# Scan in fixed steps with operands a step ahead, and full-row low products of rotated queries

## The chip, the cores and the metric

The kernel runs on one core of one Trainium2 chip. The time is the device time of one execution in microseconds (us), and the figure given for a kernel is the median of several runs. The engines of the core are named as in the profile: PE is TensorE (PEld is its weight load), DVE is VectorE, ACT is ScalarE, POOL is GpSimd, SP is the queue on which this kernel issues all its DMAs.

## The reference, cut to what matters

One encoder layer is applied to two sequences, of 512 and 1024 rows (1536 in all), of width 1024, in float32. Each has an attention branch with 8 heads (128 columns without and 64 with a rotary turn) and a bidirectional state-space scan with 32 heads in 4 groups, in chunks of 128 rows. The two parts that the change touches are these:

```python
# scan, once forward and once on the flipped sequence; per chunk c, group g, head e of the group
a_cum = jnp.cumsum(a, axis=2)
diff = acl[..., :, None] - acl[..., None, :]
Lm = jnp.exp(jnp.where(tri, diff, -jnp.inf))
CB = jnp.einsum('bclgn,bcsgn->bcgls', Cc, Bc)
y_diag = jnp.einsum('bcgls,bcgels,bcsgep->bclgep', CB, Lm, xdt)
states = jnp.einsum('bclgn,bclge,bclgep->bcgepn', Bc, decay_states, xdt)
hstate = dec * hstate + st                     # from chunk to chunk
y_off = jnp.einsum('bclgn,bcgepn,bclge->bclgep', Cc, prev, jnp.exp(a_cum))
y = y_diag + y_off + xf * D
# attention scores, per head and block of 128 queries
q = concat([q[..., :128], rope(q[..., 128:])]);  k = concat([k[..., :128], rope(k[..., 128:])])
sc = einsum('bqhd,bkhd->bhqk', q, k) * scale;  p = softmax(sc)
```

## The kernel before

Matrix products are made from a high part and a low part of each operand (`fp32r`): `mm3` (L91) issues high by high, high by low and low by high. The work runs in these stages: a start up to some 90 us, then for each of the four groups g the input products and a convolution (`conv_block`), **the scan of the group**, and the products of the gate z (`zev`); then **attention** from some 1640 us to 2260 us; then the output products.

The scan of a group (L616 to L785) has four phases. `prepass` goes backward over the chunks of the first sequence and stores each backward state in DRAM (`sbD`); `mainpass` goes forward over its 4 chunks in steps of half a chunk (4 heads, index u), 8 steps; in between, and after, `prepass` of the second sequence; then `mainpass` of the second sequence, 8 chunks in 16 steps. A step of `mainpass` holds:

- `head`: loads a chunk's transposed rows `xb` and backward state `sb`, makes the product of B and C in PSUM (`sm`) and masks it twice on DVE into `cu`.
- `weights`: two DMAs bring rows of cumulated decays (`ab`), POOL subtracts (L704, L705), ACT scales `cu` eight times (L710, L711), DVE adds, picks by a mask (L713), ACT takes the exponential (L714), DVE multiplies (L715) into `wt`.
- `products`: eight products of `wt` into `py`, one step after `weights`.
- `state` and `follow`: DVE weighs the chunk (`tmp`), ACT and POOL make high and low parts (POOL L685, L687), and a step later PE multiplies them (`mm3` into `sm`) and DVE advances the forward state `stf`.
- `decays` and `carried`: DMAs of `eb` and its exponential on ACT (L662); a step later the states times C (L673, into `sm`), multiplied by `eb` on DVE (L674).
- `tail`: DVE adds `py` and `eb` into `xs`.

All small PSUM results share the three buffers `sm`. Between steps `feed(FEED)` issues independent work, the *filler*: windows of 24 products of the input projection (`mm<-hH,wh`, lines L92 to L94) that the attention and output stages need later; 18 windows in group 0 and 21 in each of the others. A planner orders the instructions of each engine from the order in the program and its own estimate of when operands are ready. The queues are in order on the chip: an instruction that waits holds all that stands behind it on its engine.

In attention, `scores` makes for each block of queries and each 512 keys five products into one PSUM buffer `sp` (L996 to L1000): three `mm3`-like ones of the 128 plain columns, and two of the rotated ones. There the high part `xh` has 128 rows, the 64 rotated columns twice, against `kx`, which holds the high part of the keys in rows 0 to 63 and their low part in rows 64 to 127. The low part `xl` has 64 rows, against rows 0 to 63 of `kx`.

Of the kernel before, what the change touches and what calls it, by code (L numbers as in the profile page):

```python
# [9 lines left out]
F32 = mybir.dt.float32  # L10
# [18 lines left out]
G = 4  # L29
E = 8  # L30
HH = 4
FEED = 0.9
GI = 2
ASC = 0.85
VLAG = 2
HLEAD = 1
FL = 1

ORDER = "l0 a0 n0 l1 a1 m00 n1 w m01 l2 b00 b10 m10 m11 n2 b01 b11 m20 m21 b02 b12"

CUTS = (1, 7, 14, 21, 28)
DOFF = 0
COFF = 1
TH0 = 4
LT0 = 2
AL0 = 1
# [23 lines left out]
def _body(nc, tc, A, O):  # L70
# [232 lines left out]
            pass  # L303

    def tmp(name="tmp"):
        return dict(tmp=pS, ft=pre0).get(name, p1).tile([P, W], F32, name=name, bufs=1 if name == "tmp" else 2)

    free = [kd]

# [264 lines left out]
    for g in range(G):  # L574
# [12 lines left out]
        def tok(c, name, bufs):  # L587

            cs_ = slice(c * P, (c + 1) * P)
            px = smp.tile([P, W], F32, name="sm")  # L590
            for i in range(4):
                PE.transpose(out=px[:, i * P:(i + 1) * P], in_=xs[i][:, cs_], identity=ident)
            pb = smp.tile([P, P], F32, name="sm")
            PE.transpose(out=pb, in_=Bt[:, cs_], identity=ident)
            xb = pS.tile([P, W + P], F32, name=name, bufs=bufs)
            S.copy(xb[:, :W], px)
            S.copy(xb[:, W:], pb)
            return xb
# [15 lines left out]
            return new  # L614

        def prepass(o, n):  # L616
            c0, c1 = o // P, (o + n) // P
            st = None
            for c in range(c1 - 1, c0, -1):
                xb = tok(c, "xp", 1)  # L620
                nc.sync.dma_start(out=xbD[g][c], in_=xb)
                xd = weighted(xb[:, :W], 1, c)
                ps = smp.tile([P, W], F32, name="sm")
                PE.matmul(ps, lhsT=xb[:, W:], rhs=xd, start=True, stop=True)
                st = advance(st, ps, 1, c, p1.tile([P, W], F32, name="raw0", bufs=1) if st is None else st)
                nc.sync.dma_start(out=sbD[g][c - 1], in_=st)
                yield

        def mainpass(o, n):
# [24 lines left out]
            def decays(c):  # L654
                eb = {}
                for d in [0] * (c > c0) + [1] * (c < c1 - 1):
                    eb[d] = pS.tile([P, 4, P], F32, name="eb", bufs=2)
                    r0 = 32 * d + 8 * g
                    for j in range(2):
                        nc.sync.dma_start(out=eb[d][j * 64:j * 64 + 64],  # L660
                                          in_=arD[c][r0:r0 + 8, :].rearrange("(i j) l -> j i l", j=2)[j].partition_broadcast(64))
                    S.activation(eb[d], eb[d], AF.Exp)  # L662
                stt[c]["eb"] = eb

            def carried(c):

                cs_ = slice(c * P, (c + 1) * P)
                eb = stt[c]["eb"]
                for d in sorted(eb):
                    st = stt[c]["sb" if d else "sf"]  # L670
                    ps = smp.tile([P, 4, P], F32, name="sm")
                    for i in range(4):
                        PE.matmul(ps[:, i, :], lhsT=st[:, i * P:(i + 1) * P], rhs=Ct[:, cs_], start=True, stop=True)  # L673
                    V.tensor_tensor(eb[d], eb[d], ps, op=ALU.mult)  # L674
                if len(eb) == 2:
                    V.tensor_tensor(eb[1], eb[1], eb[0], op=ALU.add)
                stt[c]["off"] = eb[max(eb)]
# [16 lines left out]
                    mm3(ps, *stt[c]["parts"], True, True)  # L694
                    sf[0] = advance(sf[0], ps, 0, c, pS.tile([P, W], F32, name="stf", bufs=2))

            def weights(c, u):
                cu = stt[c]["cu"]
                e0 = u * HH
                ab = pS.tile([P, 2, HH, P], F32, name="ab", bufs=3)  # L700
                for d in range(2):
                    r0 = 32 * d + 8 * g + e0
                    nc.sync.dma_start(out=ab[:, d], in_=arD[c][r0:r0 + HH, :].partition_broadcast(P))
                GP.tensor_tensor(ab[:, 0], ab[:, 0], ac_[:, 0, c, e0:e0 + HH].unsqueeze(2).broadcast_to([P, HH, P]), op=ALU.subtract)  # L704
                GP.tensor_tensor(ab[:, 1], ab[:, 1], ac_[:, 1, c, e0:e0 + HH].unsqueeze(2).broadcast_to([P, HH, P]), op=ALU.subtract)  # L705
                wt = pS.tile([P, HH, P], F32, name="wt", bufs=3)
                t1 = pS.tile([P, HH, P], F32, name="t1", bufs=2)
                dc = [[dt_[:, d, c, e0 + e:e0 + e + 1] for e in range(HH)] for d in range(2)]
                for e in range(HH):
                    S.activation(t1[:, e], cu[:, 1, :], AF.Copy, scale=dc[1][e])  # L710
                    S.activation(wt[:, e], cu[:, 0, :], AF.Copy, scale=dc[0][e])  # L711
                V.tensor_tensor(wt, wt, t1, op=ALU.add)
                V.copy_predicated(ab[:, 0], maskb.unsqueeze(1).broadcast_to([P, HH, P]), ab[:, 1])  # L713
                S.activation(ab[:, 0], ab[:, 0], AF.Exp)  # L714
                V.tensor_tensor(wt, ab[:, 0], wt, op=ALU.mult)  # L715
                stt[c, u] = wt

# [19 lines left out]
            for i in range(4):  # L737
                xo = xs[i][:, o:o + n]
                V.tensor_scalar(xo, xo, dsum[:, 4 * g + i:4 * g + i + 1], None, op0=ALU.mult)
            for i in range(len(us) + 1):  # L740
                if i < len(us):
                    c, u = us[i]
                    if u == nu - HLEAD and c + 1 < c1:
                        head(c + 1)
                    weights(c, u)
                    if u == 0:
                        state(c)
                    if u == FL:
                        follow(c)
                    if u == DOFF:  # L750
                        decays(c)
                    if u == COFF:
                        carried(c)
                if i >= 1:
                    c, u = us[i - 1]
                    products(c, u)
                    if u == nu - 1:
                        tail(c)
                yield

        def filling():
# [11 lines left out]
                next(fill, None)  # L773

        for _ in prepass(*SEQS[0]):
            pass
        pre = prepass(*SEQS[1])
        for i, _ in enumerate(mainpass(*SEQS[0])):
            if i % 2:
                next(pre, None)  # L780
            feed(FEED)
        for _ in pre:
            pass
        for _ in mainpass(*SEQS[1]):
            feed(FEED)  # L785
        for _ in fill:
# [168 lines left out]
    def scores(u):  # L955
# [18 lines left out]
        def turn_r():  # L974
            qrw, qrr, rq, rqn = QR[si, hd // 2, w]
            xh = p2.tile([P, W], F32R, name="xh", bufs=2)
            xl = p2.tile([64, W], F32R, name="xl", bufs=2)
            pk = spp.tile([P, W], F32, name="sp")
            for b in range(4):
                PE.transpose(out=pk[:, b * P:(b + 1) * P], in_=qrr[:, b, h], identity=ident)  # L980
            S.copy(xh, pk)
            sub(xl, pk[0:64], r32(xh[0:64]))
            st["x"] = (xh, xl)
            PT[u] = []
            st["su"] = p2.tile([P, nw, 4], F32, name="su", bufs=4)

        def block(b):
            (nh, nl), (xh, xl) = st["n"], st["x"]
            rq, rqn = QR[si, hd // 2, w][2:]
            bs = slice(b * P, (b + 1) * P)  # L990
            sm = p2.tile([P, 8], F32, name="smx", bufs=8)
            sps = []
            for k in range(nw):
                out = spp.tile([P, W], F32, name="sp")
                kh, kl, kx = KV[si, hd, k][:3]
                PE.matmul(out, lhsT=nh[:, bs], rhs=kh, start=True, stop=False)  # L996
                PE.matmul(out, lhsT=nh[:, bs], rhs=kl, start=False, stop=False)  # L997
                PE.matmul(out, lhsT=nl[:, bs], rhs=kh, start=False, stop=False)  # L998
                PE.matmul(out, lhsT=xh[:, bs], rhs=kx, start=False, stop=False)  # L999
                PE.matmul(out, lhsT=xl[:, bs], rhs=kx[0:64], start=False, stop=True)  # L1000
                V.reduce_max(sm[:, k:k + 1], out, axis=AX.X)  # L1001
                sps.append(out)
            if nw == 2:
                V.scalar_tensor_tensor(sm[:, 2:3], sm[:, 0:1], sm[:, 1:2], rqn[:, b, h:h + 1], op0=ALU.max, op1=ALU.mult)  # L1004
            else:
                V.tensor_tensor(sm[:, 2:3], sm[:, 0:1], rqn[:, b, h:h + 1], op=ALU.mult)
            pp = [p2.tile([P, W], F32, name="pp", bufs=10) for _ in range(nw)]
            for k in range(nw):
                S.activation(pp[k], sps[k], AF.Exp, bias=sm[:, 2:3], scale=rq[:, b, h:h + 1], accum_out=st["su"][:, k, b:b + 1])  # L1009
            PT[u].append(pp)  # L1010
# [241 lines left out]
```

## Time and profile before

| | us |
|---|---|
| median of 3 runs | 2793.45 |
| lowest and highest | 2792.09, 2795.47 |
| the profiled execution | 2798.78 |
| its span, first to last instruction | 2797.0 |

The profile is of one execution. Busy time of an engine is the union of its instructions. Matmuls overlap in the pipeline and their ends are modelled, so the distance from the start of one matmul to the start of the next says more of what one costs than its duration.

### The profile page before, as it was taken

Reading aid. Unit: us, or ns where it says so; the run is one execution under the profiler, and the core shown is the slowest. Engines: PE = TensorE matmul, PEld = TensorE weight load, DVE = VectorE, ACT = ScalarE, POOL = GpSimd, SP = SyncE. Lnnn points to the kernel's source line nnn. Section 1 sums busy time; section 2 is a strip of 40 time slices with the busy share of each in tenths; the row PEclk is TensorE's granted clock in tenths of the full one; section 3 lists DMA queues with packets and bytes.
Section 4 is the critical chain, followed back from the end, with each engine's and each line's share of the span. In section 5 each row is a group of like instructions: output and inputs, shape, how many; then the busy total and the mean of one; then the engine's idle time right before and its main releaser. Section 6 shows DMA issues by size and latency. Waiting matters only on the chain. (4 is left out here: it accounts for less than half of the span.)

```text
span 2797.0 us, 36365 instructions
## 1 busy us (share of the span) xinstructions
PE 2658.6 (95%) x12810; PEld 2076.5 (74%) x12810; DVE 1853.7 (66%) x2962; ACT 1323.1 (47%) x2954; POOL 509.0 (18%) x455
## 2 busy tenths in 40 slices
PE   6998889999899998999988999999999999999999
PEld 2786667866778766778667877777777778888887
DVE  5877875788747777567868568776676653466631
ACT  5445554465525555564645356655565552111110
POOL 1003430034300125100224023322221200000000
PEclk9999999999999999999999999999999999999999
DMA  7236652166622366451556222211111142245433
GB/s 245 85 87 180 187 158 96 31 183 193 174 67 83 108 185 176 136 166 42 163 172 169 91 95 86 78 39 41 33 31 31 61 159 94 79 140 162 126 126 102
DMA packets 211206, 325.87 MB, mean 117 GB/s; under 512 B 24816, under 2 KB 74064, under 8 KB 210256
## 3 DMA queue, kind: packets, MB, share of 16 engines
q1 hardware_dynamic: 211024, 323.55, 38.4%
q8 instruction: 101, 1.65, 0.2%
q14 instruction: 81, 0.66, 0.1%
HBM read 245.56 MB, written 77.91 MB: 116 GB/s over the span
## 5 line engine op out<-in xcount | busy, mean ns | idle before, releaser
L92 PE MATMUL mm<-hH,wh 128*128 128x512 f32 x1656 | 669.1, 404 | 5.2 <-ACT hH L222 3.5
L94 PE MATMUL mm<-hH,wl 128*128 128x512 f32 x1656 | 657.2, 397 | 1.5 <-DVE wl L89 1.5
L93 PE MATMUL mm<-hL,wh 128*128 128x512 f32 x1656 | 656.7, 397 | 2.0 <-DVE hL L223 2.0
L92 PEld LDWEIGHTS mm<-hH,wh 128*128 128x128 f32 x1656 | 314.1, 190 | 92.2 <-issue 20.0
L93 PEld LDWEIGHTS mm<-hL,wh 128*128 128x128 f32 x1656 | 314.2, 190 | 73.5 <-issue 8.3
L94 PEld LDWEIGHTS mm<-hH,wl 128*128 128x128 f32 x1656 | 313.8, 190 | 72.9 <-issue 5.1
L93 PE MATMUL mm<-lo,wh 128*128 128x512 f32 x768 | 298.8, 389 | 0.0
L92 PE MATMUL mm<-hi,wh 128*128 128x512 f32 x768 | 298.8, 389 | 0.0
L94 PE MATMUL mm<-hi,wl 128*128 128x512 f32 x768 | 298.7, 389 | 0.0
L89 DVE TENSOR_TENSOR wl<-ws,wh 128x512 fp32r<-128x512 f32 x210 | 147.0, 702 | 127.2 <-ACT wh L230 77.4
L365 ACT CAST wh<-ws 128x512 fp32r<-128x512 f32 x72 | 44.9, 624 | 327.3 <-PE mm L93 311.9
L704 POOL TENSOR_TENSOR ab<-ab,dg 128x512 f32<-128x512 f32 x96 | 122.0, 1271 | 402.5 <-DMA ab<-arD 287.6
L365 ACT CAST ph<-tp 128x512 fp32r<-128x512 f32 x160 | 94.9, 595 | 157.3 <-PE tp L1043 157.2
L92 PEld LDWEIGHTS mm<-hi,wh 128*128 128x128 f32 x768 | 144.2, 188 | 30.1
L94 PEld LDWEIGHTS mm<-hi,wl 128*128 128x128 f32 x768 | 144.2, 188 | 29.8
L93 PEld LDWEIGHTS mm<-lo,wh 128*128 128x128 f32 x768 | 144.2, 188 | 29.8
L711 ACT ACTIVATE wt<-cu,dg 128x128 f32<-128x128 f32 x384 | 149.3, 390 | 22.1 <-DVE cu L650 22.1
L1001 DVE TENSOR_REDUCE smx<-sp 128x1 f32<-128x512 f32 x160 | 109.8, 688 | 64.3 <-PE sp L1000 63.1
L710 ACT ACTIVATE t<-cu,dg 128x128 f32<-128x128 f32 x384 | 147.7, 390 | 8.3 <-DVE cu L651 8.3
L1009 ACT ACTIVATE pp<-sp,smx,rq 128x512 f32<-128x512 f32 x160 | 123.8, 780 | 42.7 <-DVE smx L1004 29.2
L685 POOL TENSOR_TENSOR btl<-xb,bth 128x128 fp32r<-128x128 f32 x40 | 29.6, 739 | 628.7 <-ACT bth L684 626.8
L567 DVE SCALAR_TENSOR_TENSOR xs<-raw,cwh,xs 128x511 f32<-128x511 f32 (+3 forms) x128 | 129.7, 1021 | 17.4 <-ACT xs L563 14.7
(294 smaller groups left out, 5177.3 us busy)
## 6 DMA issues: line engine op xcount, KB each, us to landing
ab<-arD SPq DMA_DIRECT2D x192, 256.0 KB
ws<-w_in SPq DMA_DIRECT2D x140, 256.0 KB
eb<-arD SPq DMA_DIRECT2D x160, 128.0 KB
xbD<-xp SPq DMA_DIRECT2D x40, 320.0 KB
xb<-xbD SPq DMA_DIRECT2D x40, 320.0 KB
yT<-xs SPq DMA_DIRECT2D x48, 256.0 KB
sg<-yT SPq DMA_DIRECT2D x48, 256.0 KB
tg<-tga SPq DMA_DIRECT2D x48, 256.0 KB
```

The costliest lines, as they stand in the source:

```text
L89: V.tensor_tensor(out, a, b, op=ALU.subtract)
L92: PE.matmul(out, lhsT=ah, rhs=bh, start=first, stop=False)
L93: PE.matmul(out, lhsT=ah, rhs=bl, start=False, stop=False)
L94: PE.matmul(out, lhsT=al, rhs=bh, start=False, stop=last)
L365: S.copy(hi, src)
L567: V.scalar_tensor_tensor(acc[:, lo:hi], raw[:, lo + d:hi + d], cwh[:, 24 + 24 * k + tix:24 + 24 * k + tix + 1], acc[:, lo:hi], op0=ALU.mul ...
L685: GP.tensor_tensor(bl, stt[c]["bt"], r32(bh), op=ALU.subtract)
L704: GP.tensor_tensor(ab[:, 0], ab[:, 0], ac_[:, 0, c, e0:e0 + HH].unsqueeze(2).broadcast_to([P, HH, P]), op=ALU.subtract)
L710: S.activation(t1[:, e], cu[:, 1, :], AF.Copy, scale=dc[1][e])
L711: S.activation(wt[:, e], cu[:, 0, :], AF.Copy, scale=dc[0][e])
L1001: V.reduce_max(sm[:, k:k + 1], out, axis=AX.X)
L1009: S.activation(pp[k], sps[k], AF.Exp, bias=sm[:, 2:3], scale=rq[:, b, h:h + 1], accum_out=st["su"][:, k, b:b + 1])
```

## The change

In the scan: `prepass` makes a chunk's transposed rows and weighted rows one step before their product, with two buffers `xp` and two `tmp` in place of one, and `feed` runs after each of its steps too. It now takes one step beside each step of the first `mainpass`, not beside every other. In `mainpass`, the DMAs of `weights` become `distances`, issued two steps ahead; the rest of `weights` runs one step ahead, but for its last multiplication, which becomes `weigh` at the start of the step; `head` of the next chunk moves from the second step of a chunk to the end of the first; the exponential of `eb` moves from `decays` to `carried`. The order within a step is `weigh`, `distances`, `products`, `follow` and `carried`, `tail`, `weights`, `state`, `decays`, `head`. `FEED` goes from 0.9 to 0.66 windows a step, over 32 steps of a group where there were 26.

In attention: `xl` has 128 rows, and L1000 multiplies it with all of `kx`; this adds the product of both low parts.

```diff
-FEED = 0.9
+FEED = 0.66
...
-        return dict(tmp=pS, ft=pre0).get(name, p1).tile([P, W], F32, name=name, bufs=1 if name == "tmp" else 2)
+        return dict(tmp=pS, ft=pre0).get(name, p1).tile([P, W], F32, name=name, bufs=2)
...
-            for c in range(c1 - 1, c0, -1):
-                xb = tok(c, "xp", 1)
-                nc.sync.dma_start(out=xbD[g][c], in_=xb)
-                xd = weighted(xb[:, :W], 1, c)
-                ps = smp.tile([P, W], F32, name="sm")
-                PE.matmul(ps, lhsT=xb[:, W:], rhs=xd, start=True, stop=True)
-                st = advance(st, ps, 1, c, p1.tile([P, W], F32, name="raw0", bufs=1) if st is None else st)
-                nc.sync.dma_start(out=sbD[g][c - 1], in_=st)
+            ahead = None
+            for c in range(c1 - 1, c0 - 1, -1):
+                now = None
+                if c > c0:
+                    xb = tok(c, "xp", 2)
+                    nc.sync.dma_start(out=xbD[g][c], in_=xb)
+                    now = (c, xb, weighted(xb[:, :W], 1, c))
+                if ahead:
+                    cc, xb, xd = ahead
+                    ps = smp.tile([P, W], F32, name="sm")
+                    PE.matmul(ps, lhsT=xb[:, W:], rhs=xd, start=True, stop=True)
+                    st = advance(st, ps, 1, cc, p1.tile([P, W], F32, name="raw0", bufs=1) if st is None else st)
+                    nc.sync.dma_start(out=sbD[g][cc - 1], in_=st)
+                ahead = now
                 yield
...
-                    S.activation(eb[d], eb[d], AF.Exp)
                 stt[c]["eb"] = eb
...
                 eb = stt[c]["eb"]
+                for d in sorted(eb):
+                    S.activation(eb[d], eb[d], AF.Exp)
...
-                V.tensor_tensor(wt, ab[:, 0], wt, op=ALU.mult)
-                stt[c, u] = wt
+                stt[c, u] = [ab, wt]
+
+            def weigh(c, u):
+                ab, wt = stt[c, u]
+                V.tensor_tensor(wt, ab[:, 0], wt, op=ALU.mult)
+                stt[c, u] = wt
...
+            distances(*us[0])
+            distances(*us[1])
+            weights(*us[0])
+            yield
             for i in range(len(us) + 1):
                 if i < len(us):
-                    c, u = us[i]
-                    if u == nu - HLEAD and c + 1 < c1:
+                    weigh(*us[i])
+                if i + 2 < len(us):
+                    distances(*us[i + 2])
+                if i >= 1:
+                    products(*us[i - 1])
+                if i < len(us) and us[i][1] == 1:
+                    follow(us[i][0])
+                    carried(us[i][0])
+                if i >= 1 and us[i - 1][1] == nu - 1:
+                    tail(us[i - 1][0])
+                if i + 1 < len(us):
+                    weights(*us[i + 1])
+                if i < len(us) and us[i][1] == 0:
+                    c = us[i][0]
+                    state(c)
+                    decays(c)
+                    if c + 1 < c1:
                         head(c + 1)
-                    weights(c, u)
-                    if u == 0:
-                        state(c)
-                    if u == FL:
-                        follow(c)
-                    if u == DOFF:
-                        decays(c)
-                    if u == COFF:
-                        carried(c)
-                if i >= 1:
-                    c, u = us[i - 1]
-                    products(c, u)
-                    if u == nu - 1:
-                        tail(c)
                 yield
...
         for _ in prepass(*SEQS[0]):
-            pass
+            feed(FEED)
         pre = prepass(*SEQS[1])
-        for i, _ in enumerate(mainpass(*SEQS[0])):
-            if i % 2:
-                next(pre, None)
+        for _ in mainpass(*SEQS[0]):
+            next(pre, None)
             feed(FEED)
         for _ in pre:
-            pass
+            feed(FEED)
...
-            xl = p2.tile([64, W], F32R, name="xl", bufs=2)
+            xl = p2.tile([P, W], F32R, name="xl", bufs=2)
...
-            sub(xl, pk[0:64], r32(xh[0:64]))
+            sub(xl, pk, r32(xh))
...
-                PE.matmul(out, lhsT=xl[:, bs], rhs=kx[0:64], start=False, stop=True)
+                PE.matmul(out, lhsT=xl[:, bs], rhs=kx, start=False, stop=True)
```

## Rows read from the trace of the kernel before

**Rows 1.** The page: busy time and share of the span.
```profile
span 2797.0 us, 36365 instructions
PE 2658.6 (95%) x12810; PEld 2076.5 (74%) x12810; DVE 1853.7 (66%) x2962; ACT 1323.1 (47%) x2954; POOL 509.0 (18%) x455
```

**Rows 2.** Windows, the four scans: length, busy by engine, granted clock, DMA share, GB/s.
```profile
193.90:398.60 204.70, 179.34 (x943) 136.10 (x943) 162.13 (x227) 117.22 (x313) 76.22 (x63) 0.97 0.64 182
564.30:771.70 207.40, 189.09 (x991) 145.15 (x989) 169.14 (x240) 119.22 (x317) 79.48 (x66) 0.97 0.66 188
943.20:1158.30 215.10, 191.12 (x991) 147.18 (x989) 159.44 (x224) 120.58 (x320) 75.56 (x62) 0.95 0.63 179
1339.30:1554.10 214.80, 192.57 (x989) 147.81 (x989) 160.53 (x227) 120.08 (x318) 73.86 (x62) 0.94 0.59 173
sum 842.00, PE 752.12 PEld 576.24 DVE 651.24 ACT 477.10 POOL 305.12; mean PE 188.03 PEld 144.06 DVE 162.81 ACT 119.27 POOL 76.28
```

**Rows 3.** Windows, attention: first sequence, then second (same columns).
```profile
1640.00:1800.00 160.00, 156.50 (x912) 127.20 (x912) 128.83 (x324) 109.95 (x292) 64.82 (x65) 1.00 0.28 85
1800.00:2260.00 460.00, 454.79 (x2367) 341.35 (x2367) 314.14 (x660) 259.99 (x657) 99.16 (x103) 1.00 0.13 39
```

**Rows 4.** Timeline of PE in attention: start, duration, line, operation, operands.
```profile
1906.73 0.39 PE L998 MATMUL sp<-kh,nl 128*128 128x512 f32 x1
1906.96 0.40 PE L999 MATMUL sp<-kx,xh 128*128 128x512 f32 x1
1907.29 0.50 PE L1000 MATMUL sp<-kx,xl 64*128 64x512 f32 x1
1907.72 0.50 PE L996 MATMUL sp<-kh,nh 128*128 128x512 f32 x1
1908.05 0.40 PE L997 MATMUL sp<-kl,nh 128*128 128x512 f32 x1
1908.29 0.39 PE L998 MATMUL sp<-kh,nl 128*128 128x512 f32 x1
```

**Rows 5.** Line L1000: counts and durations in ns (min, median, max).
```profile
L1000 PEld LDWEIGHTS sp<-kx,xl x160: 182/183/187, 1667.6 to 2257.2; 64*128 64x128 f32 x160
L1000 PE MATMUL sp<-kx,xl x160: 393/498/502, 1667.6 to 2257.2; 64*128 64x512 f32 x160
```

**Rows 6.** Timeline of weight loads around the same products.
```profile
1906.73 0.19 PEld L999 LDWEIGHTS sp<-kx,xh 128*128 128x128 f32 x1
1907.28 0.18 PEld L1000 LDWEIGHTS sp<-kx,xl 64*128 64x128 f32 x1 [0.36 <-issue]
```

**Rows 7.** Line L89 in attention: DVE's low parts with 128 and 64 rows.
```profile
L89 DVE TENSOR_TENSOR pl<-tp,ph x152: 671/690/693, 1679.9 to 2259.0; 128x512 fp32r<-128x512 f32 x152
L89 DVE TENSOR_TENSOR xl<-sp,xh x24: 671/673/683, 1666.3 to 2241.6; 64x512 fp32r<-64x512 f32 x24
```

**Rows 8.** Waits of PE, whole span: us in total, times, longest.
```profile
PE sm L673 <- DVE cu L651: 34.4, 15, 5.1
PE sm L93 <- POOL zt L687: 25.0, 19, 4.5
...
PE sm L624 <- DVE tmp L602: 15.3, 10, 4.4
PE py L726 <- DVE wt L715: 8.5, 6, 2.7
```

**Rows 9.** Waits of the other engines, whole span.
```profile
POOL ab L704 <- DMA ab<-arD: 287.6, 53, 74.2
...
ACT ab L714 <- DVE ab L713: 136.3, 62, 4.6
...
ACT eb L662 <- DMA eb<-arD: 66.0, 36, 5.4
```

**Rows 10.** Windows in the last scan: a low-clock stretch, then a full-clock one.
```profile
1451.50:1458.30 6.80, 6.36 (x25) 5.06 (x26) 4.47 (x7) 2.64 (x8) 2.39 (x3) 0.50 0.15 32
...
1461.00:1468.00 7.00, 7.00 (x38) 5.69 (x38) 6.10 (x6) 5.03 (x15) 5.93 (x5) 1.00 0.72 214
```

**Rows 11.** Groups on ACT in the second scan: busy, mean ns, idle before.
```profile
L662 ACT ACTIVATE eb<-eb 128x512 f32<-128x512 f32 x18 | 11.2, 624 | 15.1 <-DMA eb<-arD 15.1
```

More of the change, by code (lines that the diff above doesn't have):

```diff
@@ L35 @@
 VLAG = 2
-HLEAD = 1
-FL = 1
 ORDER = "l0 a0 n0 l1 a1 m00 n1 w m01 l2 b00 b10 m10 m11 n2 b01 b11 m20 m21 b02 b12"
 CUTS = (1, 7, 14, 21, 28)
-DOFF = 0
-COFF = 1
 TH0 = 4
@@ L695, in follow, with distances @@
                     sf[0] = advance(sf[0], ps, 0, c, pS.tile([P, W], F32, name="stf", bufs=2))
-            def weights(c, u):
-                cu = stt[c]["cu"]
+            def distances(c, u):
                 e0 = u * HH
@@ L703, in weights @@
                     nc.sync.dma_start(out=ab[:, d], in_=arD[c][r0:r0 + HH, :].partition_broadcast(P))
-                GP.tensor_tensor(ab[:, 0], ab[:, 0], ac_[:, 0, c, e0:e0 + HH].unsqueeze(2).broadcast_to([P, HH, P]), op=ALU.subtract)
-                GP.tensor_tensor(ab[:, 1], ab[:, 1], ac_[:, 1, c, e0:e0 + HH].unsqueeze(2).broadcast_to([P, HH, P]), op=ALU.subtract)
+                stt[c, u] = [ab]
+            def weights(c, u):
+                cu = stt[c]["cu"]
+                e0 = u * HH
+                ab, = stt[c, u]
+                for d in range(2):
+                    GP.tensor_tensor(ab[:, d], ab[:, d], ac_[:, d, c, e0:e0 + HH].unsqueeze(2).broadcast_to([P, HH, P]), op=ALU.subtract)
                 wt = pS.tile([P, HH, P], F32, name="wt", bufs=3)
                 t1 = pS.tile([P, HH, P], F32, name="t1", bufs=2)
-                dc = [[dt_[:, d, c, e0 + e:e0 + e + 1] for e in range(HH)] for d in range(2)]
                 for e in range(HH):
-                    S.activation(t1[:, e], cu[:, 1, :], AF.Copy, scale=dc[1][e])
-                    S.activation(wt[:, e], cu[:, 0, :], AF.Copy, scale=dc[0][e])
+                    S.activation(t1[:, e], cu[:, 1, :], AF.Copy, scale=dt_[:, 1, c, e0 + e:e0 + e + 1])
+                    S.activation(wt[:, e], cu[:, 0, :], AF.Copy, scale=dt_[:, 0, c, e0 + e:e0 + e + 1])
                 V.tensor_tensor(wt, wt, t1, op=ALU.add)
```

## The prediction

> **What bounds the kernel now.** I read the page first, then busy time by stage, then within the two stages that the diff touches who made PE wait, and at last what one product costs there.
>
> On the page PE is busy for 95% of the span, far ahead of any other engine [rows 1]. That share is a mean over stages, so it doesn't say where the missing 138 us (2797.0 - 2658.6) lie. The windows do: the four scans last 842 us together with PE busy for 752, so 90 of the idle microseconds lie there, and the granted clock is 0.94 to 0.97 instead of 1.00 [rows 2]. DVE is busy for 651 of these 842 us, 77%. In attention PE is idle for 3.5 of 160 and 5.2 of 460 us at full clock, and DVE is busy for 81% and 68% [rows 3]. So attention is bound by what PE is given to do, and only shorter PE work helps; the scans are bound by latencies between engines, with PE and then DVE as floors beneath.
>
> **Attention: full rows for `xl`.** The count of products does not change, 160 before and after [rows 5]. What changes is how the 64-row product sits among its neighbours [rows 4]. A full-row product is followed by the next after 0.23 us (1906.73 to 1906.96) or 0.24 (1908.05 to 1908.29). Around L1000 the steps are 0.33 (L999 to L1000), 0.43 (L1000 to L996) and 0.33 (L996 to L997): 1.09 us for three, where three full-row ones take some 0.70. So each 64-row product costs 0.39 us more than its place. The weight loads show why [rows 6]: the load of L999 starts together with the product before its own, a step ahead, while that of L1000 starts 0.36 us after its predecessor ended, level with its own product at 1907.29; so nothing of it is hidden, and the load after it pays likewise. Whatever follows L1000 pays this, a product or a transpose; I take 0.39 for all.
>
> With 128 rows L1000 has the shape of L999, whose spacing among full-row neighbours the same rows show. So 160 x 0.39 = 62 us of PE time goes: 32 of the 160 in the first sequence (12 us), 128 in the second (50). What lies beside it: ACT and DVE work stays. In the second sequence DVE's 314 us would then stand in 410, 77%, so I take nine tenths of 50, 45 us; in the first its 129 us would stand in 148, 87%, so half of 12, 6 us. Together **51 us**; the bounds are 62 (all of it) and 30 (DVE and the five `sp` buffers hold PE for half). DVE's `xl` gets twice the rows; the same operation takes 690 ns with 128 rows and 673 with 64 [rows 7], 24 of them, 0.4 us in all: nothing, hidden under PE, and 0.4 us without that cover.
>
> There is a rule against this part. The Trainium skill, in "TensorE: Matmul & The Clock Gate", section "LDWEIGHTS (loading the stationary operand)" and its closing table, says that a weight load costs by its columns and not by its rows, and that a single product of few rows takes as long as a full one. By it the edit is worth nothing, and the sum below would come to 2748 us. For the load alone the trace agrees (183 ns with 64 rows, 0.19 us with 128 [rows 5, 6]), but the spacing [rows 4] does not.
>
> **Scan: where PE waits.** Four chains hold PE there [rows 8]: the fourth small product of a chunk waits for DVE to finish masking `cu`, since all share three `sm` buffers (34.4 us); the second product of `follow` for POOL's low part (25.0); the product of `prepass` for DVE's `tmp` (15.3); `products` for DVE's last multiplication (8.5). By part of the change:
>
> - `head` a step earlier. `cu` is masked a step before `carried` needs the buffer: the 34.4 go. What is late next is in the rivals.
> - `prepass` a step ahead, with two `xp` and `tmp`: `tmp` is ready a step before its product, the 15.3 go. Its DMAs are the same in number and size.
> - `weights` a step ahead and `weigh` before `products` by a step: the 8.5 go. POOL's and ACT's work is unchanged.
> - `distances` two steps ahead: POOL waits 287.6 us in all for these rows [rows 9]. POOL works only some 36% of the scans (305 of 842 [rows 2]), so this idle time costs nothing itself, but `state`'s parts stand behind these subtractions on POOL. An earlier `ab` lets them go sooner. On the other side, `follow` still comes one step after `state`, with a smaller filler between (0.66 windows, not 0.9). I take half of 25.0, **12.5 us**; bounds 0 and 25.
> - The exponential of `eb` to `carried`: ACT no longer stops for the DMA (66.0 us of waits [rows 9]); ACT works 57% of the scans, so only what stands behind profits, and that is counted above. But it now lies right before DVE's reading of the `sm` buffers. Its price is bounded below by 0 (ACT is there in time) and above by ACT's wait for DVE's pick before each exponential of `ab`, which stands ahead of it on ACT: 2.2 us mean (136.3 / 62 [rows 9]) per chunk, 48 chunks, 106 us. One such exponential takes 0.62 us [rows 11] and a chunk has up to two, 1.25 us; part of that is covered by PE's filler. I take 0.8 us per chunk, nearer the bare work than the wait: 48 x 0.8 = **38 us given back**.
> - `FEED` and the steps: the same 81 windows in 128 steps instead of 104, and none of the last steps of a group without filler. That moves PE work and adds none; I cost it at zero, its cover being that PE has a window to do whenever the scan's chain is late. Without this cover, a step costs what its chain takes, which is the 90 us of idle time that are already there.
>
> Removed: 34.4 + 15.3 + 8.5 + 12.5 = 71 us. The clock adds to it. Its mean says that some 72 us of the scans ran at the lower level (twice the missing share: 2 x (0.03 x 204.7 + 0.03 x 207.4 + 0.05 x 215.1 + 0.06 x 214.8) [rows 2]), which is 1.2 GHz, the 0.50 of a single such stretch, where PE did 25 products in 6.8 us against 38 in 7.0 at 2.4 GHz [rows 10]. PE stood waiting before or in such stretches. If it was always busy there, that cost half of 72, 36 us. With most named waits gone I take a third back, 12 us; bounds 0 and 36. So 71 + 12 - 38 = **45 us** from the scans.
>
> **Sum.** The profiled execution took 2798.8 us, its span plus 1.8. 2798.8 - 51 - 45 = 2702.8; the median of the runs is 5.3 us under that execution, so **2697 us**.
>
> **Rivals.**
>
> *B: the scans gain nothing.* DVE is the second floor: in the first `mainpass` it gets a step of `prepass` beside each step, and its queue is in order, so waits only change their names. For it: DVE's 77% is an average, and its waits are spread over all chains of rows 8. Against it: `cu` is late for its place in the queue, not for DVE's load. Only attention's 51 is left: 2742 us.
>
> *C: the scans reach PE's busy time.* All 90 us go [rows 2]: 2793.5 - 51 - 90 = 2652, and less if the clock's 36 us return too. For it: the largest waits of rows 8 are all attacked. Against it: DVE at 651 of 752 us would be 87% busy with hardly a wait left.
>
> *D: full rows bring nothing.* A product of few rows costs as much as a full one, and the 0.39 us belong to something else around L1000, such as its being the last into its buffer. Then only the scans gain: 2793.5 - 45 = 2748. For it: the loads take the same time [rows 5, 6]. Against it: the step before L1000 is already 0.33 us, and the gap is in the load [rows 6]. (This is what the skill's rule above would give.)
>
> *E: slower.* The exponential of `eb` behind that of `ab` on ACT holds two of three `sm` buffers, so PE's next small product waits in every chunk. It decides from (83 + 51) / 48 = 2.8 us per chunk; the longest wait of rows 9 is 4.6, the mean 2.2. Halfway between 2.8 and 4.6, at 3.7, the time is 2793.5 + 178 - 134 = 2837. Against it: fillers can stand between.
>
> **Chances.** The forecast 0.50, its own range 2670 to 2725; B 0.24; C 0.17; D 0.05; E 0.04. The bounds of attention (30 to 62) and of the scans (0 to 90, with some of the clock) give 2640 to 2764. A range of 2640 to 2758 leaves out E, the lower third of C and the upper fifth of B, 0.15 together. A measurement of this kernel can tell about 0.2%, 5.6 us; faster by more than that are A to D, 0.95; within it 0.01; slower 0.04.
>
> **What would show it.** In attention: L1000 with 128 rows, steps of 0.23 us throughout a block, and 51 us less between the same products. In the scans: no row of PE waiting for `cu`, `tmp` or `wt`; `follow`'s wait for POOL halved; a new row of PE waiting in `sm` for DVE's L674 (or its line now), up to 38 us; the clock nearer to 1.00. Wrong would be: PE's idle time in attention growing by tens of microseconds, or the scans still at 205 to 215 us with other names in the waits.

## The result, and the profile after

The changed kernel takes 2715.7 us (median of 4 runs, 2709.8 to 2718.3) against 2793.8 us before, measured beside it: ratio 0.9718, 95% interval 0.9701 to 0.9734, 78 us. 2697 us were predicted. Its page begins so:

```profile
span 2714.4 us, 36314 instructions
PE 2586.5 (95%) x12810; PEld 2080.5 (77%) x12810; DVE 1833.5 (68%) x2962; ACT 1322.6 (49%) x2954; POOL 505.1 (19%) x455
```

PE's share is the same 95% as in [rows 1], of a span 82.6 us shorter: both the work of PE and its idle time shrank. By stage, first the four scans (windows, columns as in [rows 2]):

```profile
197.00:384.00 187.00, 170.49 (x921) 130.99 (x921) 155.47 (x223) 115.55 (x312) 73.54 (x63) 0.96 0.70 197
554.60:746.50 191.90, 178.86 (x967) 137.86 (x965) 165.82 (x239) 117.75 (x315) 79.47 (x67) 0.98 0.71 202
923.50:1125.20 201.70, 183.07 (x967) 141.09 (x965) 153.11 (x222) 118.55 (x317) 73.97 (x62) 0.95 0.66 189
1310.10:1507.80 197.70, 180.66 (x965) 139.28 (x965) 151.74 (x227) 118.52 (x316) 74.63 (x62) 0.97 0.64 187
sum 778.30, PE 713.09 PEld 549.22 DVE 626.14 ACT 470.38 POOL 301.62; mean PE 178.27 PEld 137.31 DVE 156.54 ACT 117.59 POOL 75.41
```

They fell from 842.0 to 778.3 us, but not all of this is gain. Each window holds some 24 products of PE fewer than in [rows 2] (967 for 991): one window of filler per group now runs behind the scan, some 5.4 us. Attention starts at 1599.1 us and not at 1640.0, which is 40.9 us earlier; the other 22.8 us of the 63.7 went to the stages between. Of the scans' own gain PE's idle time is 24.7 us (89.9 to 65.2).

Attention in two windows (columns as in [rows 3]; the last score product of the first sequence lies some 6 us before the cut between them):

```profile
1599.10:1760.00 160.90, 153.60 (x958) 136.97 (x959) 135.03 (x333) 114.89 (x304) 66.57 (x67) 0.99 0.29 87
1760.00:2188.00 428.00, 411.32 (x2380) 352.64 (x2378) 316.76 (x662) 261.77 (x656) 98.97 (x101) 1.00 0.14 44
```

It lasts 588.9 us, where it lasted 630.2 (1640.0 to its last product at 2270.2). PE's busy time there fell from 621.0 us (all of 1640.0 to 2270.2, ten microseconds more than [rows 3] show) to 564.9, and its idle time rose from 9 to 24 us. Cut behind the last score product of the first sequence (at 1800.6 us before, 1753.9 after), the first sequence is 5.8 us shorter (160.6 to 154.8) and the second 35.6 (469.7 to 434.1); in the second PE's busy time fell by 46.6 us, and its idle time grew from 5.7 to 16.7. A score block in PE's timeline (the lines of `scores` have moved by 16, so L1015 and L1016 were L999 and L1000):

```profile
1901.50 0.39 PE L1015 MATMUL sp<-kx,xh 128*128 128x512 f32 x1
1901.72 0.39 PE L1016 MATMUL sp<-kx,xl 128*128 128x512 f32 x1
1901.95 0.39 PE L1012 MATMUL sp<-kh,nh 128*128 128x512 f32 x1
1902.18 0.39 PE L1013 MATMUL sp<-kl,nh 128*128 128x512 f32 x1
1902.40 0.39 PE L1014 MATMUL sp<-kh,nl 128*128 128x512 f32 x1
```

The steps of 0.33, 0.43 and 0.33 us of [rows 4] are 0.22, 0.23 and 0.23 now.

The waits of PE (us in total, times, longest) answer to [rows 8]. In the new numbering L677 and L654 are the old L673 and L651, L89 in `sm` with L691 the old L93 with L687, L626 the old L624, L738 with L727 the old L726 with L715; L588 and L590 are the transposes of `tok`, L678 is the multiplication by `eb`, the old L674:

```profile
PE sm L677 <- DVE cu L654: 21.8, 7, 4.8
...
PE sm L89 <- POOL zt L691: 14.3, 10, 3.2
PE sm L626 <- DVE eb L678: 9.0, 4, 3.4
...
PE sm L651 <- ACT xb L592: 4.8, 3, 2.1
PE sm L590 <- DVE eb L678: 4.5, 5, 1.3
...
PE py L738 <- DVE wt L727: 2.9, 3, 1.6
...
PE sm L626 <- ACT xp L592: 1.7, 1, 1.7
```

The four waits of before, 83.2 us, are 39.0 now; the wait for `tmp` is gone, that for POOL is nearly halved, but that for `cu`, which should have gone, is still there with 21.8 us. New names stand below it, 13.5 us of them waits for the multiplication by `eb`, 4.8 for `xb`; at L626 itself `xp` holds 1.7.

### The profile page after: what moved, and what is told of

The parts are those of the page before. It is cut to its first block, busy times and chain, and to the rows that moved or that the text cites. A ratio compares the mean times of both kernels' runs of the same rounds, so it can differ in the third digit from the quotient of the medians.

```text
span 2714.4 us, 36314 instructions
## 1 busy us (share of the span) xinstructions
PE 2586.5 (95%) x12810; PEld 2080.5 (77%) x12810; DVE 1833.5 (68%) x2962; ACT 1322.6 (49%) x2954; POOL 505.1 (19%) x455
## 5 line engine op out<-in xcount | busy, mean ns | idle before, releaser
L89 PE MATMUL mm<-hL,wh 128*128 128x512 f32 x1656 | 662.0, 400 | 3.6 <-DVE hL L219 3.6
L89 PEld LDWEIGHTS mm<-hL,wh 128*128 128x128 f32 x1656 | 315.4, 190 | 77.3 <-issue 10.2
L714 POOL TENSOR_TENSOR ab<-ab,dg 128x512 f32<-128x512 f32 x192 | 236.9, 1246 | 418.5 <-DMA ab<-arD 293.4
L89 PE MATMUL mm<-lo,wh 128*128 128x512 f32 x768 | 298.8, 389 | 0.0
L85 DVE TENSOR_TENSOR wl<-ws,wh 128x512 fp32r<-128x512 f32 x210 | 151.3, 722 | 134.4 <-ACT wh L226 86.7
L89 PEld LDWEIGHTS mm<-lo,wh 128*128 128x128 f32 x768 | 144.1, 188 | 29.9
L719 ACT ACTIVATE wt<-cu,dg 128x128 f32<-128x128 f32 x384 | 141.3, 391 | 46.5 <-DVE cu L653 46.1
L718 ACT ACTIVATE t<-cu,dg 128x128 f32<-128x128 f32 x384 | 137.3, 390 | 2.6 <-DVE cu L654 2.4
L721 DVE COPY_PREDICATED ab<-maskb,ab 128x512 f32<-128x512 uint8 x96 | 86.4, 905 | 69.3 <-POOL ab L714 69.3
```

The lines of the kernel that those rows point to most:

```text
L85: V.tensor_tensor(out, a, b, op=ALU.subtract)
L89: PE.matmul(out, lhsT=ah, rhs=bl, start=False, stop=False)
L714: GP.tensor_tensor(ab[:, d], ab[:, d], ac_[:, d, c, e0:e0 + HH].unsqueeze(2).broadcast_to([P, HH, P]), op=ALU.subtract)
L718: S.activation(t1[:, e], cu[:, 1, :], AF.Copy, scale=dt_[:, 1, c, e0 + e:e0 + e + 1])
L719: S.activation(wt[:, e], cu[:, 0, :], AF.Copy, scale=dt_[:, 0, c, e0 + e:e0 + e + 1])
```

## The experiments

All runs are given beside the kernel before on the same chip; the intervals are of the ratio to it. The chips differ from one set of runs to the next, so runs of different sets are compared by their ratios.

**The two parts apart.** `rows_only` is the kernel before with the three lines of attention; `scan_only` is the changed kernel without them.

```diff
 # rows_only, on the kernel before
-            sub(xl, pk[0:64], r32(xh[0:64]))
+            sub(xl, pk, r32(xh))
...
-                PE.matmul(out, lhsT=xl[:, bs], rhs=kx[0:64], start=False, stop=True)
+                PE.matmul(out, lhsT=xl[:, bs], rhs=kx, start=False, stop=True)
```

> The kernel before with the attention part of the change alone: xl with 128 rows, the last product of a score block with all of kx. Theory (a 64-row product among 128-row ones costs its unhidden weight load, and attention is bound by PE): attention shortens from 630 to about 589 us as in the changed kernel, the rest stays, so 2793.8 - 41 = 2753 us, between 2747 and 2759. The prediction's own term, 51 us, would give 2743. Rival (rows cost nothing, attention of the changed kernel was shortened by the other order of work): 2794.

> The changed kernel with the 64-row xl of the kernel before: the scan part alone. If the two parts add up, it saves what rows_only doesn't: 78 - 41 = 37 us, 2757 us, with attention back at 630 us and the four scans at 778 us. Rival (the scan part gains more alone and the parts overlap): under 2745. Rival (the scan's shorter length is only filler moved behind it): 2790, since one window of 5.5 us in each group now lies behind the scan.

Measured: `rows_only` 2751.9 us, ratio 0.9856 (0.9834 to 0.9879); `scan_only` 2755.1 us, 0.9867 (0.9844 to 0.9889). The product of the two ratios is 0.9725, and the whole change has 0.9718: the parts add up. Attention is 586.3 us in the first and 632.1 in the second, as the theory had it.

**What a 64-row product costs.** `two_short` gives the product before it 64 rows too, so that two such products are neighbours.

```diff
-                PE.matmul(out, lhsT=xh[:, bs], rhs=kx, start=False, stop=False)
+                PE.matmul(out, lhsT=xh[0:64, bs], rhs=kx[0:64], start=False, stop=False)
```

> The kernel before with the product of the high part xh cut to 64 rows as well (rows 0 to 63 of xh and kx), so two neighbouring products of a score block have 64 rows; this leaves out the high by low product of the rotated columns. Theory A (the cost is the change between 64 and 128 rows, twice per block, wherever it stands): the step between the two short products is the plain 0.23 us and the time stays at 2794 +- 6 us. Theory B (every 64-row product pays for its own load): the step between them is 0.43 us, 160 x 0.2 = 32 us more, 2826 us. Theory C (short products are cheaper side by side): under 2785.

Measured: 2793.4 us, ratio 1.0010 (0.9997 to 1.0023): the second short product costs nothing more. PE's timeline of this kernel:

```profile
1902.89 0.40 PE L998 MATMUL sp<-kh,nl 128*128 128x512 f32 x1
1903.22 0.50 PE L999 MATMUL sp<-kx,xh 64*128 64x512 f32 x1
1903.56 0.39 PE L1000 MATMUL sp<-kx,xl 64*128 64x512 f32 x1
1903.88 0.50 PE L996 MATMUL sp<-kh,nh 128*128 128x512 f32 x1
1904.21 0.40 PE L997 MATMUL sp<-kl,nh 128*128 128x512 f32 x1
1904.45 0.39 PE L998 MATMUL sp<-kh,nl 128*128 128x512 f32 x1
```

Four steps of 0.32 to 0.34 us stand where [rows 4] had 0.23, 0.33, 0.43 and 0.33: 1.32 us both times. So theory A holds in its sum, though not in its detail, since I had expected a plain step between the two. The pattern fits a price for each change of the row count, some 0.1 us on the step into the changed product and 0.1 on the step after it: two changes lie around one short product (0.33, 0.43, 0.33) or around two (four times 0.33).

**Parts of the scan undone, one at a time,** each from the changed kernel.

```diff
 # head_late: head(c + 1) moved from the end of a chunk's first step
+                    if us[i][1] == 1 and us[i][0] + 1 < c1:
+                        head(us[i][0] + 1)
                     weigh(*us[i])
 # exp_early: in decays again, and not in carried
+                    S.activation(eb[d], eb[d], AF.Exp)
 # dist_late: distances(i + 1) right before weights(i + 1), no distances(i + 2)
+                    distances(*us[i + 1])
                     weights(*us[i + 1])
 # pre_same: xp and tmp with one buffer
+                ahead = now
                 if ahead:
```

> The changed kernel with head of the next chunk back at the start of a chunk's second step, all else as changed. Theory of the prediction (masking cu a step earlier frees the small PSUM buffer in time): PE's wait for cu goes from 21.8 back towards 34 us or more, the scans gain 13 to 25 us, 2729 to 2741 us. Rival (the waits for cu that are left are a late DVE queue, held by POOL's late subtraction, wherever head stands): 2716 +- 6 us.

> The changed kernel with the exponential of eb back in decays, right behind its DMAs. Theory of the prediction (the exponential in carried delays DVE's reading of the small PSUM buffers): PE's new waits for L678 in L626 and L590, 13.5 us, go, 2703 us or less, down to 2680 if the whole 38 us of the prediction were there. Rival (ACT then stops for the DMA of eb and holds the parts of state and the scalings behind it): ACT's wait for eb rises from 52 us, 2725 to 2745 us.

> The changed kernel with distances issued right before weights of the same half chunk, not a step earlier still. Theory (SP's queue is in order, so the lead lets POOL start on time): POOL's waits for ab rise, follow waits longer for POOL, 2730 to 2755 us. Rival (the three ab buffers already let the DMA start no earlier than it did, or the planner issues it as early as a buffer is free): 2716 +- 6 us.

> The changed kernel with prepass as before in itself: product in the same step as its operands, one xp and one tmp buffer; the filler and the steps stay as changed. Theory (a step of lead is what hides DVE's tmp): PE's wait for tmp comes back, 15 us, 2731 us or a little more. Rival (filler between the steps of prepass hides it as well): 2716 +- 6 us.

| | median us | ratio to before | 95% interval |
|---|---|---|---|
| changed kernel | 2715.7 | 0.9718 | 0.9701 to 0.9734 |
| `head_late` | 2724.4 | 0.9756 | 0.9741 to 0.9770 |
| `exp_early` | 2713.0 | 0.9720 | 0.9700 to 0.9740 |
| `dist_late` | 2709.3 | 0.9700 | 0.9685 to 0.9714 |
| `pre_same` | 2718.3 | 0.9735 | 0.9716 to 0.9754 |

Only `head` shows a price of its own, some 9 us (by the ratios 11). It doesn't come by the way that the theory named, since PE's wait for `cu` rises by 3.4 us only and new waits of `products` stand beside it (waits of PE in `head_late`):

```profile
PE sm L677 <- DVE cu L654: 25.2, 18, 2.5
...
PE py L738 <- ACT t L718: 11.0, 3, 4.0
PE py L738 <- DVE wt L727: 10.4, 7, 2.6
```

The exponential's place and the longer lead of the DMAs show no price. In `exp_early` neither expectation came true: the waits for L678 stay, and ACT's wait for `eb` is 45.7 us where it was 52.3. In `dist_late` POOL's wait for `ab` did not rise (279.4 us for 293.4), and PE's for POOL is 13.4 where it was 14.3. The lead of `prepass` shows no price beyond the interval; none of the four is faster than the changed kernel by more than the intervals allow. Yet in `pre_same` the wait that I had priced did come back (waits of PE):

```profile
PE sm L677 <- DVE cu L654: 22.6, 8, 5.6
...
PE sm L627 <- DVE tmp L598: 16.3, 18, 1.9
PE sm L89 <- POOL zt L691: 14.3, 9, 3.5
```

Its four scans, as the sum of their windows:

```profile
sum 780.80, PE 706.49 PEld 543.95 DVE 641.47 ACT 471.11 POOL 300.42; mean PE 176.62 PEld 135.99 DVE 160.37 ACT 117.78 POOL 75.10
```

Its 16.3 us for `tmp` are the 15.3 of [rows 8], and the kernel is 2.6 us slower by medians, 5 by the ratios. PE's idle time in the scans is 74.3 us (780.8 - 706.5) where the changed kernel has 65.2, so 9 of the 16 us show as idle time. PE's busy time is 6.6 us shorter on the other side, with the lower clock level held for some 47 us of the scans by the granted clock of the windows, not 55, and the two profiled executions last the same (2714.3 and 2714.4 us). With one profiled execution of each, what the lead of `prepass` is worth stays open between 0 and some 10 us.

**Pace and order.** `old_pace` is the changed kernel with the old distribution of filler and `prepass` steps; `new_pace` is `rows_only` with the new one.

```diff
 # old_pace, on the changed kernel (new_pace: the reverse, on rows_only, with FEED = 0.73)
-FEED = 0.66
+FEED = 0.9
...
-            feed(FEED)
+            pass
         pre = prepass(*SEQS[1])
-        for _ in mainpass(*SEQS[0]):
-            next(pre, None)
+        for i, _ in enumerate(mainpass(*SEQS[0])):
+            if i % 2:
+                next(pre, None)
             feed(FEED)
         for _ in pre:
-            feed(FEED)
+            pass
```

> The changed kernel with the old pace: FEED 0.9, no filler between the steps of the first prepass, one step of the second prepass beside every other step of the first mainpass and the rest alone after it; the order within a step and the leads stay as changed. Theory 1 (the gain of the scans is the even pace: the filler, the prepass steps): most of the 37 us go, 2740 to 2752 us. Theory 2 (the gain is the order within a step, weights a step ahead and weigh, head early): 2716 +- 8 us. Both in part: in between.

> The kernel before with full rows in attention and the new pace alone: a step of prepass beside every step of the first mainpass, filler between the steps of prepass too, FEED 0.73 so that 29 steps take the 21 windows; order and leads within a step stay as before. Beside it stands rows_only with 2752 us. Theory 1 (pace): 2716 to 2728 us. Theory 2 (order): 2752 +- 8 us.

Measured: `old_pace` 2720.1 us, 0.9732 (0.9712 to 0.9753); `new_pace` 2730.4 us, 0.9776 (0.9753 to 0.9798). Seen from `rows_only` (0.9856), the new pace alone brings 22 us by the ratios, the new order alone 35, and both together 39, each to some 9 us by the intervals. The first run is as theory 2 has it, the second is not: the order alone does nearly all, and the pace alone still more than half. `new_pace` does it with PE still waiting 44.5 us for `cu`, more than before. The four scans, as sums of their windows, of `new_pace` and then of `old_pace`:

```profile
sum 798.80, PE 719.29 PEld 554.20 DVE 655.55 ACT 473.08 POOL 302.37; mean PE 179.82 PEld 138.55 DVE 163.89 ACT 118.27 POOL 75.59
sum 806.30, PE 733.51 PEld 559.35 DVE 629.87 ACT 477.38 POOL 301.68; mean PE 183.38 PEld 139.84 DVE 157.47 ACT 119.35 POOL 75.42
```

In PE's idle time the two parts nearly add: it was 89.9 us before [rows 2] and is 79.5 with the pace alone, 72.8 with the order alone and 65.2 with both. The clock does not add: by the granted clock of their windows (0.95 to 0.98) its lower level held for some 72 us before, and for 52 to 56 us in all three. These are single executions; the pace itself (filler in `prepass`, its steps, `FEED`) was not taken apart.

**Is it the buffers, or the queue of DMAs?** Three attempts at what is left.

```diff
 # sm4_mm2: small PSUM buffers 4, those of the input products 2
-    mmp = pool("mmp", bufs=3, space=PSUM)
-    smp = pool("smp", bufs=3, space=PSUM)
+    mmp = pool("mmp", bufs=2, space=PSUM)
+    smp = pool("smp", bufs=4, space=PSUM)
 # eb4, on pre_same
-                    eb[d] = pS.tile([P, 4, P], F32, name="eb", bufs=2)
+                    eb[d] = pS.tile([P, 4, P], F32, name="eb", bufs=4)
 # ab_act: the DMAs of distances
-                    nc.sync.dma_start(out=ab[:, d], ...)
+                    nc.scalar.dma_start(out=ab[:, d], ...)
```

> The changed kernel with four small PSUM buffers sm and two buffers mm for filler, z and input products, in place of three and three. Theory (PE waits in the scans because the three sm buffers are all held while DVE is late): waits for cu, eb and stf in sm, some 40 us, fall by half, scans 20 us shorter, less what the input products lose with two buffers: 2690 to 2710 us. Rival (the next product in line needs what DVE or POOL is late with anyway): scans unchanged, 2716 us or more.

> pre_same (2718 us) with four eb buffers in place of two; the space comes from the single xp and tmp. Theory (the waits that are left start on SP: the DMAs of eb wait for tail to free a buffer, those of ab behind them land late, POOL subtracts late, DVE's queue stands, cu is masked late): with a free buffer SP does not stop, PE's waits for POOL (14.3 us) and cu (22.6) fall by half or more, 2695 to 2705 us. Rival (POOL or DVE are late by their own load): 2718 +- 6 us.

> The changed kernel with the DMAs of ab (distances) issued on ACT's queue instead of SP's. Theory (what PE still waits for in the scans, follow for POOL and carried for cu, goes back to POOL waiting for ab, whose DMA stands on SP behind those of eb, xb and sb that wait for buffers): POOL's wait for ab falls by at least a third, PE's 21.8 and 14.3 us of waits for cu and POOL by half, 2716 - 15 = 2700 us. Rival (ACT's own queue then holds the issue, or ACT is held by it; the waits change their names): 2716 or up to 20 us more.

`sm4_mm2`: 2713.0 us, 0.9709 (0.9687 to 0.9730), the same as the changed kernel within the intervals. Its waits of PE, and the sum of its scans' windows, show what became of `cu`:

```profile
PE sm L89 <- POOL zt L691: 34.2, 21, 4.6
...
PE mm L90 <- DVE wl L85: 10.9, 9, 2.4
PE sm L626 <- DVE eb L678: 6.2, 7, 1.6
...
PE py L738 <- DVE wt L727: 4.6, 4, 2.0
...
sum 765.90, PE 703.54 PEld 546.20 DVE 631.63 ACT 467.26 POOL 303.21; mean PE 175.89 PEld 136.55 DVE 157.91 ACT 116.81 POOL 75.80
```

The wait for `cu` is gone, all 21.8 us; the wait for POOL, next in PE's order, has grown by 19.9, and PE's idle time in the scans is 62.4 us where it was 65.2. The run also takes a buffer from `mm`, and PE's wait for `wl` grows from 1.2 to 10.9 us, so it doesn't show a fourth `sm` buffer by itself. `eb4`: 2731.6 us, 0.9779 (0.9760 to 0.9799), slower than `pre_same`. Beside `pre_same`, on which it is built, POOL's wait for `ab` in the scans fell from 183.3 us to 162.4 (the lists say 206.9 and 239.9, with waits of 23.6 and 77.5 us between the third and the fourth scan). PE's wait for POOL fell from 14.3 to 9.9, less than the half that the theory wants, the one for `cu` hardly (22.6 to 21.8), and those for `tmp` and `stf` grew to 21.0 and 12.8. Why it is slower was not found. `ab_act`: 2769.9 us, 0.9919 (0.9896 to 0.9943), 54 us slower than the changed kernel: ACT's waits for the DMA of `eb` went from 52.3 to 151.7 us, and POOL's for `ab` rose from 293.4 to 318.3. The rival held in kind, and the price was more than it said; why ACT then waits so long for `eb` wasn't taken apart.

One stall of the changed kernel's last scan, read through four queues, shows how such waits hang together. SP (start, duration, line):

```profile
1444.20 3.08 SPq L663 DMA_DIRECT2D eb<-arD  x4
1447.39 1.00 SPq L706 DMA_DIRECT2D ab<-arD  x2
```

The two DMAs of `ab` stand behind four of `eb`. POOL, whose first two subtractions came after 6.62 us of waiting for them (the 181st and 182nd on both lines):

```profile
1451.72 3.79 POOL L714 TENSOR_TENSOR ab<-ab,dg 128x512 f32<-128x512 f32 x2 [6.62 <-DMA ab<-arD]
1455.47 0.45 POOL L689 TENSOR_TENSOR btl<-xb,bth 128x128 fp32r<-128x128 f32 x1
1455.88 1.72 POOL L691 TENSOR_TENSOR zt<-tmp,zt 128x512 fp32r<-128x512 f32 x1
1457.56 2.48 POOL L714 TENSOR_TENSOR ab<-ab,dg 128x512 f32<-128x512 f32 x2
```

DVE, where the two masks of `cu` (L653, L654) stand behind two picks (L721) that wait for POOL, and behind the filler's low part (L85) that waits for ACT; on ACT its cast (L226, at 1461.43) stands behind an exponential (L722) that waited 3.73 us for the second pick:

```profile
1455.54 0.97 DVE L721 COPY_PREDICATED ab<-maskb,ab 128x512 f32<-128x512 uint8 x1 [1.93 <-POOL ab L714]
...
1460.07 0.73 DVE L721 COPY_PREDICATED ab<-maskb,ab 128x512 f32<-128x512 uint8 x1 [1.93 <-POOL ab L714]
1462.07 1.15 DVE L85 TENSOR_TENSOR wl<-ws,wh 128x512 fp32r<-128x512 f32 x1 [1.26 <-ACT wh L226]
...
1463.73 0.28 DVE L653 TENSOR_TENSOR cu<-sm,cmat 128x128 f32<-128x128 f32 x1
...
1464.53 0.28 DVE L654 TENSOR_TENSOR cu<-sm,cmat 128x128 f32<-128x128 f32 x1
```

And PE, whose product for `cu` (L651) was made at 1453.04, over ten microseconds before DVE masked it:

```profile
1453.04 0.49 PE L651 MATMUL sm<-ch,kd 128*128 128x128 f32 x2
...
1457.65 0.80 PE L89 MATMUL sm<-zt,bth 128*128 128x512 f32 x1 [3.10 <-POOL zt L691]
...
1464.87 1.01 PE L677 MATMUL sm<-ch,sb 128*128 128x128 f32 x3 [3.90 <-DVE cu L654]
```

PE's two waits, for POOL and for `cu`, go back here to one source, a subtraction on POOL that began late because its DMAs did. This is how taking one name off the list can move the time to the next. This is one stall that was read; that it is the rule for all of them was not shown.

## Why the prediction was right, and where not

The range and the sign held, and the stages are as forecast: attention 41 us shorter (51 said), the scans with the filler that moved behind them 41 (45 said). So rivals B (no gain in the scans), C (all 90 us) and E (slower) fell. By step:

- *A 64-row product among full ones costs 0.39 us.* That it costs is shown by `rows_only` and `two_short`. The full 62 us were 56 in PE's busy time, 0.35 us for each of the 160. The reason that I gave, an unhidden weight load of the short product, is only half of it: a second short product has no further price, so the price is of the change of rows.
- *Nine tenths of it come through in the second sequence.* This is the term that was mis-sized: 36 us came through of the 50, seven tenths, with 11 us of new idle time on PE there. The first sequence gave its 6 us as said. Over both, 15 us of new idle time took 56 down to 41. In PE's waits of attention the largest are for `pl`, `pp` and `gt`, 17 us together where they were 3, which DVE and ACT finish later than the shorter PE work wants them.
- *Full rows bring nothing* (rival D) fell: 39 us by `rows_only`, against the rule of the Trainium skill, "TensorE: Matmul & The Clock Gate", "LDWEIGHTS (loading the stationary operand)" and closing table, that a weight load goes by its columns and a single product of few rows takes as long as a full one. For the load alone the changed trace still agrees with it, 188 ns where it was 183; for products in a row the measurement decides, and the rule leaves out what a change of rows costs its neighbours.
- *The wait for `cu` goes.* Failed: 21.8 us are left, and without it (`sm4_mm2`) POOL's takes its place. The early `head` is worth some 9 us (`head_late`), not 34, and PE's wait for `cu` rises there by 3.4 us only.
- *`tmp` and `wt` go, POOL's wait halves.* As waits, yes: no row of PE waiting for `tmp`, 2.9 us for `wt`, 14.3 for POOL (12.5 said). But the lead of `distances`, to which I gave POOL's half, is not its cause: without it the wait is 13.4 (`dist_late`), and with the old order and the new pace it is 2.3 (`new_pace`). As time, for `tmp` at most in part: `pre_same` brings its 16 us of waiting back, with 9 us more of idle time in the scans, and takes 3 us longer by medians, 5 by the ratios, inside the intervals. `weights` a step ahead with `weigh` was not undone alone.
- *38 us given back for the exponential in `carried`.* Failed: `exp_early` is as fast. The waits on the multiplication by `eb` stay there as well (14.4 us for 13.5), so they are not the exponential's.
- *`FEED` and the steps cost and bring nothing.* Failed: the pace alone is worth 22 us without the new order, and 4 with it, which is inside the intervals.
- *The clock gives 12 us back.* By the windows the lower level held for some 72 us of the scans and now for 55 (2 x (0.04 x 187.0 + 0.02 x 191.9 + 0.05 x 201.7 + 0.03 x 197.7)); half of the difference is 8.5, between one execution and one.

So it was luck that the scans' 45 us were near 41, through errors of both signs: I added up PE's waits as if each were time of its own, and took off a price that isn't there. What the gain is made of is settled to this point: 25 us are idle time of PE, some 8 us the clock; the new order alone brings nearly all of it, and the pace alone more than half. Which part of the order does it stays open, since the parts that were undone singly are worth some 10 us or less. The remaining 8 us lie in PE's busy time and were not traced.

## What to carry to other kernels

Look at the distance from start to start of neighbouring products, not only at durations: where the row count changed, a product of 64 rows cost 0.35 to 0.4 us more than its place of 0.23, and padding it with rows that were already there took that price away. Where PE waits for several engines whose queues are in order, its waits are no list of gains to be added: take one away on the chip before counting on the next. And count what a stage holds before comparing its length; a third of the scans' shorter length here was work that had moved behind them.

## What the runs showed that I had not expected

Two neighbouring 64-row products among 128-row ones cost as much as one (1.32 us for four steps, both times): the steps fit a price of 0.2 us for each change of the row count, shared by the step into the change and the one after it. And moving the DMAs of `ab` from SP to ACT, which was busy for 60% of the scans (470 of 778 us), cost 54 us.
